# Seam of a feed-forward block and a token mixer: the hand-written order of the splits, and where one head's query weights are loaded and cast

## The chip, the cores and the metric

The kernel runs on one core of a Trainium2 chip. The metric is the device time of one execution in microseconds (us). The engines are named as the profile names them: PE (matrix multiply; PEld is its weight load), DVE (vector), ACT (scalar), POOL (GpSimd, here only issuing DMAs that add into their target) and SP (issues the other DMAs). SBUF is the on-chip memory, PSUM the matmul accumulator with eight banks.

## The reference

One layer on x of shape 512 x 1024, all in float32:

```python
x = x + 0.5 * swiglu(rmsnorm(x, ffn1_norm), ffn1_w_gate, ffn1_w_up, ffn1_w_down)    # D_FF = 2816
x = x + token_mixer(rmsnorm(x, mix_norm), w_in, w_out, ...)
x = x + 0.5 * swiglu(rmsnorm(x, ffn2_norm), ffn2_w_gate, ffn2_w_up, ffn2_w_down)
return rmsnorm(x, final_norm)
```

The mixer projects the normed x by w_in to queries, keys and values of four differential heads (two softmax maps each) and eight dilated heads, attends with a bucketed position bias, and projects by w_out.

## The kernel before

**Numbers.** Every float32 operand of a matmul is split into a high part (rounded to the PE's format) and a low part (the rest). A product is three matmuls: high x high, high x low, low x high (`mm3`, L178 to L180). Such a split is one ACT instruction for the high part and one DVE instruction for the low part, which has to wait for the high part.

**First block.** Gate and up products come first, then the down product in two groups. A group multiplies 2 x 2 blocks by Strassen's scheme: seven products of block sums, and each product runs over the group's pairs of rows. The last down group has six pairs, so 42 operations, numbered 0 to 41, of 6 matmuls each (two token tiles, 128 x 512 outputs). The code's unit of time is `STEP`, one such operation. Weights of operation t are summed on DVE (`total`, L421), cast on ACT (`high`, L453) and the rest is taken on DVE (`low`, L457), nominally 5, 4 and 3 steps ahead. Results of a product are added to x by DVE (L551). Every instruction is an event with a nominal time and a rank; events are emitted in that order, and that is the program order of PE, DVE and ACT, and in this part of SP and POOL too. Each engine works through its own order.

**Closing of the block (`close`).** While the last group runs, events with times relative to its beginning load the first query/key weights of the mixer (`early_load`), split them (`early_high`, `early_low`), square the finished x for the norm (`squared`), form 1/rms (`mean`, `root_part`), scale x (`scaled`), and turn token tiles 0 and 1 by PE transposes (`turn`). A weight set (u, hf) belongs to head u and to one half hf of the eight row blocks k of 128 inputs; a part (u, hf, c) has 512 columns, for two k. Before, (0, 0) and (0, 1) are loaded into `dead` buffers, tiles of the old xh/xl that nobody reads any more, and split within the last group. (1, 0) and (1, 1) are loaded whole into two of the three `raw` buffers, which all other streamed weights use too, and split in the seam.

**The seam (`seam`).** A list of events with times in us puts DVE, ACT and PE work in order, from the end of the group through 16 query/key chunks. Chunks 0 to 3 are u = 0 on the left half of the tokens (token tiles 0 and 1), 4 to 7 are u = 1 on the left half, 8 to 11 and 12 to 15 the same on the right half. A chunk takes two k, for queries and keys: 12 matmuls of 256 columns. Ahead of chunks 4 and 5 PE turns token tiles 2 and 3, whose x needs `summed` (the last product's sums), `squared`, `mean`, `root_part` and `scaled` first. The turned x lies in PSUM, two k in a bank: `xts[side][k // 2]`. `gathered("h", ...)` is the high part of one k on one half (ACT, L1286), `gathered("l", ...)` the low part (DVE, L1288). Chunks with k need both. In the order before, the high parts of side 0 have times of their own and each low part comes 0.45 us behind its high part, so that the list alternates between neighbours:

```python
split(0, (-1.3, -0.9, -0.5, 0.3, 1.0, 1.8, 2.5, 3.2))   # high at t, low at t + 0.45
```

The steps of the mixer's own schedule (`step(c)`) are part of the list too: they load the value weights (`raw_vw`, L165), cast them on ACT (L1409) and take the rest on DVE (L1413) from step 3 on.

Of the kernel before, what the change touches and what calls it, by code (L numbers as in the profile page):

```python
# [14 lines left out]
F32 = mybir.dt.float32  # L15
F32R = mybir.dt.float32r
I32 = mybir.dt.int32
AF = mybir.ActivationFunctionType
# [3 lines left out]
P = 128  # L22
S = 512
D = 1024
FF = 2816
KD = D // P
# [78 lines left out]
STEP = 1410  # L105
# [12 lines left out]
def tile_macaron(ctx: ExitStack, tc, xs, xT, wf, wgu1, wst1, wdg1, wqk, wvw, wv, wo, wgu2, wst2,  # L118
                 wdg2, fg, lams, relb, addc, xn, out):
    nc = tc.nc  # L120
    V, A, G, T = nc.vector, nc.scalar, nc.gpsimd, nc.tensor

    ctx.enter_context(tc.manual_schedule(engines={mybir.EngineType.PE}))
    cp = ctx.enter_context(tc.tile_pool(name="cp", bufs=1))
    sl = ctx.enter_context(tc.tile_pool(name="sl", bufs=1))
    tp = ctx.enter_context(tc.tile_pool(name="tp", bufs=2))
    wp = ctx.enter_context(tc.tile_pool(name="wp", bufs=3))
# [5 lines left out]
    def slot(i, nm, dt=F32):  # L133
        return sl.tile([P, S], dt, tag=f"slot{i}", name=nm)
# [8 lines left out]
    sq = cp.tile([P, S], F32, tag="sq", name="sq")  # L143
# [4 lines left out]
    x = [None] + [cp.tile([P, S], F32, tag=f"x{k}", name=f"x{k}")[:] for k in range(1, KD)]  # L148
# [110 lines left out]
    def ffn(wgu, wst, wdg, n0, n1, norm, early, res, nm, hooks, first=None,  # L259
# [519 lines left out]
        def pipeline():  # L779
# [401 lines left out]
    eps = sp.tile([P, 1], F32, tag="eps", name="eps", bufs=1)  # L1181
    G.memset(eps[:], EPS)
    root = sp.tile([P, 1], F32, tag="root", name="root", bufs=1)
    fin = sp.tile([P, 10 * NQ], F32, tag="fin", name="fin", bufs=1)
    def number(n, tt):
        return fin[:, n * NQ + tt:n * NQ + tt + 1]

    def first_sum(tt):
        V.tensor_scalar(number(2, tt), number(0, tt), 1.0 / D, EPS, op0=ALU.mult, op1=ALU.add)

    def cast(o, a):
        A.copy(o, a)

    def rest(o, a, h):
        V.tensor_tensor(o, a, h.bitcast(F32), op=ALU.subtract)

    closing, early_w, early_raw = {}, {}, {}

    def dead(k):
        return [cp.tile([P, S], F32, tag=f"x{n}{k}", name=f"dead{n}{k}")[:] for n in "hl"]  # L1200

    def early_load(u, hf):
        if u == 0:
            early_raw[u, hf] = dead(1 + 4 * hf)
            for k in range(2):
                nc.sync.dma_start(early_raw[u, hf][k], wqk[u, hf, :, k * 512:(k + 1) * 512])
        else:
            raw = early_raw[u, hf] = wp.tile([P, 1024], F32, tag="raw", name=f"raw_q{u}{hf}")
            nc.sync.dma_start(raw[:], wqk[u, hf])

    def early_source(u, hf, c, n):
        return early_raw[u, hf][:, c:c + n] if u else early_raw[u, hf][c // 512]

    def early_high(u, hf, c, n):
        if u == 0:
            if c == 0 and hf == 0:
                closing[hf] = [tp.tile([P, 5 * HS], F32R, tag="pr0", name=f"wq{n}{hf}")[:, :1024] for n in "hl"]
            elif c == 0:
                tx = tp.tile([P, 12 * HS], F32R, tag="tx", name="wqx", bufs=1)
                closing[hf] = tx[:, :1024], tx[:, 1024:2048]  # L1220
            h, l = [part[:, c:c + n] for part in closing[hf]]
        else:
            h, l = [slot(i, f"wq{n}{u}{hf}{c}", F32R)[:] for n, i in zip("hl", EARLY_SLOTS[u, hf][c // 512])]
        for k in range(n // 256):
            o = slice(k * 256, (k + 1) * 256)
            early_w[u, hf * 4 + c // 256 + k] = h[:, o], l[:, o]
        early_raw[u, hf, c] = h, l
        cast(h, early_source(u, hf, c, n))

    def early_low(u, hf, c, n):  # L1230
        h, l = early_raw[u, hf, c]
        rest(l, early_source(u, hf, c, n), h)

    ys, xts = {}, {}

    def squared(dh, tt):
        if "junk" not in closing:
            closing["junk"] = dead(7)[0]
        junk = closing["junk"] if tt < 2 else sq[:]
        A.activation(junk, x[4 * dh + tt], AF.Square, accum_out=number(dh, tt))  # L1240
        if dh == 0:
            first_sum(tt)

    def scaled(dh, tt):
        y = tp.tile([P, S], F32, tag=("ob", "ptb")[tt % 2], name=f"y{dh}{tt}")
# [15 lines left out]

    def close(at, begin):
        last = begin + 36 * STEP
        todo = [(begin + 9 * STEP, 1.5, early_load, 0, 0), (begin + 11 * STEP, 1.5, early_load, 0, 1),
                (begin + 20.5 * STEP, 5, A.activation, root[:], eps[:], AF.Sqrt),
                (last - 1.8 * STEP, 1.6, early_load, 1, 0),
                (last + 0.4 * STEP, 1.6, early_load, 1, 1)]
        for t, part in ((16.2, (0, 0, 0, 512)), (18.6, (0, 0, 512, 512)), (21.2, (0, 1, 0, 512)), (26.2, (0, 1, 512, 512))):
            todo.append((begin + t * STEP, 4.6, early_high, *part))
            todo.append((begin + (t + 0.9) * STEP, 2.7, early_low, *part))  # L1270
        for tt in range(2):
            todo += [(begin + (25 + 0.5 * tt) * STEP, 4, squared, 0, tt),
                     (last + (0.6 + 0.5 * tt) * STEP, 4, squared, 1, tt),
                     (last + (1.3 + 0.8 * tt) * STEP, 0, mean, tt),
                     (last + (1.6 + 0.8 * tt) * STEP, 0, root_part, tt),
                     (last + (4.4 + 0.6 * tt) * STEP, 4, squared, 1, 2 + tt),
                     (last + (4 + tt) * STEP, 3.9, turn, tt)]
# [24 lines left out]
    def seam(step):  # L1302

        todo, now = [], [0.0]

        def ev(t, f, *a):
            todo.append((t, len(todo), f, a))

        def pe(cost, f, *a):
            ev(now[0], f, *a)  # L1310
            now[0] += cost

        def split(side, highs):
            for k, t in enumerate(highs):
                ev(t, gathered, "h", 1, side, k, xts)
                ev(t + 0.45, gathered, "l", 1, side, k, xts)

        def summed(tt):
            V.scalar_tensor_tensor(x[tt], closing["sums"][tt % 2], 0.5, x[tt], op0=ALU.mult, op1=ALU.add)

        for k in range(1, KD, 2):
            xh[k], xl[k] = [cp.tile([P, S], F32R, tag=f"x{n}{k}", name=f"x{n}{k}m") for n in "hl"]
        ev(-1.5, V.tensor_scalar_mul, sm[:, KD:2 * KD], sm[:, KD:2 * KD], 2.0)
        split(0, (-1.3, -0.9, -0.5, 0.3, 1.0, 1.8, 2.5, 3.2))
        for tt in range(2):
            t = (0.0, 0.9)[tt]
            ev(t, summed, 2 + tt)
            ev(t + 0.6, squared, 0, 2 + tt)
            ev(t + 1.4, mean, 2 + tt)
            ev(t + 1.9, root_part, 2 + tt)  # L1330
            for i in range(2):
                ev(t + 2.6, scaled, i, 2 + tt)
        for t, low, hf, c in ((4.0, 4.7, 0, 0), (5.2, 5.9, 0, 512), (6.6, 7.3, 1, 0), (7.4, 8.1, 1, 512)):
            ev(t, early_high, 1, hf, c, 512)
            ev(low, early_low, 1, hf, c, 512)
        for c in range(16):
            if c in (4, 5):
                pe(0.8, turn, c - 2)
            if c == 5:
                split(1, [now[0] + 0.1 + 0.42 * k for k in range(KD)])  # L1340
# [518 lines left out]
    def step(t):  # L1859
# [272 lines left out]
```

## Time and profile before

| | us |
|---|---|
| median of 3 runs | 916.54 (915.68 to 919.17) |
| the profiled execution | 918.43 |
| its span, first to last instruction | 916.7 |
| mean granted PE clock | 0.999 of full |

| engine | busy us | share of the span |
|---|---|---|
| PE | 906.6 | 99% |
| DVE | 733.4 | 80% |
| ACT | 564.5 | 62% |
| POOL | 101.7 | 11% |

In a timeline row the columns are start (us from the span's start), duration, engine, line, operation, output <- inputs, shapes and count; behind it in brackets stands the idle time of the engine before the row and what ended it. A windows row gives the stretch, its length and the busy time of PE, PEld, DVE, ACT and POOL (with instruction counts), then granted clock, DMA share and GB/s. A row of DMA issues gives target <- source, queue, count, KB each and median us from issue to landing. A count above x1 in a timeline row is of instructions merged into it. The last down group begins at 282.49 us, and the seam's first chunk at 341.46.

### The profile page before, as it was taken

How to read it: one execution, taken by the hardware profiler on the slowest of the kernel's cores; microseconds unless marked ns; L12 is line 12 of the kernel's file. 1: busy time of each engine (PE TensorE's matmuls, PEld its weight loads, DVE VectorE, ACT ScalarE, POOL GpSimd, SP SyncE). 2: the span in 40 equal slices, each digit the busy share in tenths (PEclk: the TensorE clock that was granted, in tenths of full speed). 3: DMA queues.
4: the chain of work that ended last, by engine and by line, in shares of the span. 5: the costliest groups of instructions: out<-in, count | busy, mean ns of one | idle time of the engine just before them, and what ended most of it. 6: DMA issues, size and time to landing. Idle time of an engine off the chain costs nothing.

```text
span 916.7 us, 16048 instructions
## 1 busy us (share of the span) xinstructions
PE 906.6 (99%) x5766; PEld 817.8 (89%) x5766; DVE 733.4 (80%) x1539; ACT 564.5 (62%) x1197; POOL 101.7 (11%) x127
## 2 busy tenths in 40 slices
PE   9999999999999999999999999999999999999997
PEld 7888998899998888888989878989999889999885
DVE  7697998889888876757866546788888888988885
ACT  6345765466567656655776676656666546666673
POOL 0000202121112000000000000010211112112200
PEclk9999999999999999999999999999999999999999
DMA  7464879677889623334444204364788769879902
GB/s 243 127 158 118 212 202 252 149 192 190 202 211 282 159 69 99 93 93 117 137 111 120 69 24 138 93 164 119 202 186 234 178 161 242 205 188 235 258 24 92
DMA packets 68256, 145.47 MB, mean 159 GB/s; under 512 B 7824, under 2 KB 8336, under 8 KB 68176
## 3 DMA queue, kind: packets, MB, share of 16 engines
q1 hardware_dynamic: 51744, 114.34, 39.0%
q0 software_dynamic: 16432, 30.11, 20.5%
q8 instruction: 45, 0.74, 0.3%
q14 instruction: 35, 0.29, 0.1%
HBM read 139.13 MB, written 2.14 MB: 154 GB/s over the span
## 4 chain that ended last, share of the span: by engine, by line
PE 93%; DVE 3%; DMA 2%; ACT 2%; issue 1%; SPq 0%; DVEq 0%; ACTq 0%
PE pt L179 7%; PE pt L180 7%; PE pt L178 7%; PE pwo L178 2%; PE pwo L179 2%; PE pwo L180 2%; PE pua L178 2%; PE pua L180 2%; PE pua L179 2%; PE pq L178 1%; PE pq L179 1%; PE pq L180 1%; PE pk L178 1%; PE pk L180 1%; PE pk L179 1%; PE pga L178 1%
## 5 line engine op out<-in xcount | busy, mean ns | idle before, releaser
L1625 ACT ACTIVATE pr<-pr,mx 128x128 f32<-128x128 f32 (+3 forms) x64 | 36.0, 563 | 36.7 <-DVE mx L1622 36.4
L1622 DVE CUSTOM_DVE_ANT_0 pr<-sc,strip 128x128 f32<-128x128 f32 (+3 forms) x64 | 30.5, 489 | 23.1 <-PE sc L1620 22.6
L551 DVE SCALAR_TENSOR_TENSOR x<-pt,x 128x512 f32<-128x512 f32 x50 | 33.2, 690 | 19.6 <-PE pt L180 12.3
L396 POOL DMA_DIRECT2D s1bg<-wst_dram x10 | 8.6, 862 | 326.7 <-DVE fin L1297 232.5
L457 DVE TENSOR_TENSOR w<-s2b,w 128x512 fp32r<-128x512 f32 x38 | 26.1, 687 | 8.1 <-ACT w L453 8.1
L453 ACT CAST w<-raa 128x512 fp32r<-128x512 f32 x34 | 21.0, 622 | 17.4 <-DVE raa L421 11.7
L453 ACT CAST w<-s2b 128x512 fp32r<-128x512 f32 x38 | 23.6, 620 | 7.0 <-DVE s2b L426 7.0
L453 ACT CAST w<-rab 128x512 fp32r<-128x512 f32 x28 | 17.3, 622 | 16.6 <-DVE rab L421 7.6
L178 PE MATMUL pwo<-w,mh 128*128 128x512 f32 x64 | 25.9, 405 | 0.0
L179 PE MATMUL pwo<-w,mh 128*128 128x512 f32 x64 | 25.0, 391 | 0.0
L180 PE MATMUL pwo<-w,ml 128*128 128x512 f32 x64 | 25.0, 391 | 0.0
L457 DVE TENSOR_TENSOR w<-s2a,w 128x512 fp32r<-128x512 f32 x30 | 20.6, 686 | 3.0 <-ACT w L453 2.8
L457 DVE TENSOR_TENSOR w<-raa,w 128x512 fp32r<-128x512 f32 x34 | 22.8, 686 | 0.0
L1413 DVE TENSOR_TENSOR w<-raw_qk,w 128x512 fp32r<-128x512 f32 x24 | 16.4, 687 | 7.9 <-ACT w L1409 7.8
L453 ACT CAST w<-s2a 128x512 fp32r<-128x512 f32 x30 | 18.6, 620 | 6.6 <-DVE s2a L426 5.8
L179 PE MATMUL pxgb<-ttb,w 128*128 128x256 f32 x80 | 22.5, 281 | 0.0
L396 POOL DMA_DIRECT2D s1ag<-wst_dram x8 | 7.1, 883 | 126.9 <-DMA s3ag<-wst_dram 50.7
L1619 PE MATMUL sc<-k,q 128*128 128x128 f32 (+3 forms) x64 | 20.5, 322 | 0.0
L1620 PE MATMUL sc<-l,q 128*128 128x128 f32 (+3 forms) x64 | 20.2, 322 | 0.0
L179 PE MATMUL pxub<-ttb,w 128*128 128x256 f32 x72 | 20.2, 281 | 0.0
L457 DVE TENSOR_TENSOR w<-rab,w 128x512 fp32r<-128x512 f32 x28 | 18.8, 688 | 0.0
L179 PE MATMUL pwga<-xl,w 128*128 128x256 f32 x64 | 18.0, 281 | 0.0
(1135 smaller groups left out, 3924.7 us busy)
## 6 DMA issues: line engine op xcount, KB each, us to landing
raw_qk<-wqk_dram SPq DMA_DIRECT2D x12, 512.0 KB, 3.6
raw0bg<-wst_dram SPq DMA_DIRECT2D x10, 512.0 KB, 5.1
raw0bu<-wst_dram SPq DMA_DIRECT2D x9, 512.0 KB, 5.7
raw_gua<-wgu_dram SPq DMA_DIRECT2D x8, 512.0 KB, 3.8
raw0ag<-wst_dram SPq DMA_DIRECT2D x8, 512.0 KB, 5.0
strip<-bias_rows SPq DMA_DIRECT2D x16, 256.0 KB, 3.6
raw_wo<-wo_dram SPq DMA_DIRECT2D x8, 512.0 KB, 3.6
raw0au<-wst_dram SPq DMA_DIRECT2D x7, 512.0 KB, 5.8
```

The source lines that it names most:

```text
L178: T.matmul(po, wh, mh, start=first, stop=False, skip_group_check=on)
L179: T.matmul(po, wh, ml, start=False, stop=False, skip_group_check=on)
L180: T.matmul(po, wl, mh, start=False, stop=last, skip_group_check=on)
L396: nc.gpsimd.dma_start(t[:], b, accum_op=ALU.add)
L453: A.copy(made[t][0], source(t))
L457: V.tensor_tensor(l, source(t), h.bitcast(F32), op=ALU.subtract)
L551: V.scalar_tensor_tensor(o, a, f, b, op0=ALU.mult, op1=op1)
L1413: V.tensor_tensor(l[:, c:c + 512], raw[:, c:c + 512], h[:, c:c + 512].bitcast(F32), op=ALU.subtract)
L1619: T.matmul(ps[:, :w], qs[:, qi], ks[:, :w], start=True, stop=False)
L1620: T.matmul(ps[:, :w], qs[:, qi], ls[:, :w], start=False, stop=True)
L1622: V.tensor_tensor_reduce(out=pi, in0=ps[:, :w], in1=st["b"][m][:, w - 1::-1], op0=ALU.add, op1=ALU.min, scale=1.0, scalar=3.0e38, accum_ou ...
L1625: A.activation(pi, pi, AF.Exp, scale=-1.0, bias=st["mx"][:, m, i:i + 1], accum_out=st["ls"][:, m, i:i + 1])
```

## The change

In `close`, the loads of (1, 0) and (1, 1) are cut in halves of 256 KB and three of the four go to dead buffers within the last group: (1, 0, 0) and (1, 0, 1) to the low tiles of k = 3 and 7, (1, 1, 0) to the buffer that (0, 1, 0) had. Only (1, 1, 1) keeps a `raw` buffer. Three of the four splits of u = 1 move from the seam to the last group, at steps 23.6, 28 and 38.5 (high) and 24.5, 28.9 and 39.8 (low); the fourth, (1, 1, 512), stays in the seam ahead of step 4. `EARLY_SLOTS` names other SBUF slots for the results. In `seam`, the front is one list: the two high parts of a bank, then its low parts, with the sums, squares and norm steps of token tiles 2 and 3 between them. `first_sum` becomes an entry of its own, and `dead(k)` hands out one shared pair of tiles for each k. The right half's order is unchanged.

```diff
-EARLY_SLOTS = {(1, 0): ((16, 17), (18, 19)), (1, 1): ((20, 21), (6, 7))}
+EARLY_SLOTS = {(1, 0): ((19, 20), (14, 15)), (1, 1): ((23, 0), (26, 27))}
...
     def dead(k):
-        return [cp.tile([P, S], F32, tag=f"x{n}{k}", name=f"dead{n}{k}")[:] for n in "hl"]
-
-    def early_load(u, hf):
-        if u == 0:
-            early_raw[u, hf] = dead(1 + 4 * hf)
-            for k in range(2):
-                nc.sync.dma_start(early_raw[u, hf][k], wqk[u, hf, :, k * 512:(k + 1) * 512])
+        if ("dead", k) not in closing:
+            closing["dead", k] = [cp.tile([P, S], F32, tag=f"x{n}{k}", name=f"dead{n}{k}")[:] for n in "hl"]
+        return closing["dead", k]
+
+    def early_load(u, hf, k):
+        if (u, hf, k) == (1, 1, 1):
+            r = early_raw[u, hf, k] = wp.tile([P, 1024], F32, tag="raw", name="raw_q")[:, :512]
         else:
-            raw = early_raw[u, hf] = wp.tile([P, 1024], F32, tag="raw", name=f"raw_q{u}{hf}")
-            nc.sync.dma_start(raw[:], wqk[u, hf])
...
+            r = early_raw[u, hf, k] = {(0, 0): dead(1)[k], (0, 1): dead(5)[k], (1, 0): dead((3, 7)[k])[1],
+                                       (1, 1): dead(5)[0]}[u, hf]
+        nc.sync.dma_start(r, wqk[u, hf, :, k * 512:(k + 1) * 512])
...
-        todo = [(begin + 9 * STEP, 1.5, early_load, 0, 0), (begin + 11 * STEP, 1.5, early_load, 0, 1),
-                (begin + 20.5 * STEP, 5, A.activation, root[:], eps[:], AF.Sqrt),
-                (last - 1.8 * STEP, 1.6, early_load, 1, 0),
-                (last + 0.4 * STEP, 1.6, early_load, 1, 1)]
-        for t, part in ((16.2, (0, 0, 0, 512)), (18.6, (0, 0, 512, 512)), (21.2, (0, 1, 0, 512)), (26.2, (0, 1, 512, 512))):
-            todo.append((begin + t * STEP, 4.6, early_high, *part))
-            todo.append((begin + (t + 0.9) * STEP, 2.7, early_low, *part))
+        todo = [(begin + 20.5 * STEP, 5, A.activation, root[:], eps[:], AF.Sqrt)]
+        for t, part in ((9, (0, 0, 0)), (9, (0, 0, 1)), (11, (0, 1, 0)), (11, (0, 1, 1)), (16.5, (1, 0, 0)),
+                        (17.5, (1, 0, 1)), (22.6, (1, 1, 0)), (34.2, (1, 1, 1))):
+            todo.append((begin + t * STEP, 1.5, early_load, *part))
+        for t, low, part in ((16.2, 17.1, (0, 0, 0)), (18.6, 19.5, (0, 0, 512)), (21.2, 22.1, (0, 1, 0)),
+                             (23.6, 24.5, (1, 0, 0)), (26.2, 27.1, (0, 1, 512)), (28, 28.9, (1, 0, 512)),
+                             (38.5, 39.8, (1, 1, 0))):
+            todo.append((begin + t * STEP, 4.6, early_high, *part, 512))
+            todo.append((begin + low * STEP, 2.7, early_low, *part, 512))
...
-        split(0, (-1.3, -0.9, -0.5, 0.3, 1.0, 1.8, 2.5, 3.2))
-        for tt in range(2):
-            t = (0.0, 0.9)[tt]
-            ev(t, summed, 2 + tt)
-            ev(t + 0.6, squared, 0, 2 + tt)
-            ev(t + 1.4, mean, 2 + tt)
-            ev(t + 1.9, root_part, 2 + tt)
-            for i in range(2):
-                ev(t + 2.6, scaled, i, 2 + tt)
-        for t, low, hf, c in ((4.0, 4.7, 0, 0), (5.2, 5.9, 0, 512), (6.6, 7.3, 1, 0), (7.4, 8.1, 1, 512)):
-            ev(t, early_high, 1, hf, c, 512)
-            ev(low, early_low, 1, hf, c, 512)
+        front = ("h0 h1 l0 l1 h2 h3 sum2 l2 l3 h4 h5 sq2 h6 sum3 l4 sq3 first2 mean2 l5 h7 l6 root2 l7 "
+                 "scaled2 first3 mean3 root3 scaled3")
...
+        ev(5.2, early_high, 1, 1, 512, 512)
+        ev(5.9, early_low, 1, 1, 512, 512)
```

In `front`, h and l are the high and low parts of a k on the left half; sum, sq, first, mean, root and scaled belong to token tiles 2 and 3.

More of the change, by code (lines that the diff above doesn't have):

```diff
@@ L1226, in early_high @@
             early_w[u, hf * 4 + c // 256 + k] = h[:, o], l[:, o]
-        early_raw[u, hf, c] = h, l
-        cast(h, early_source(u, hf, c, n))
+        closing[u, hf, c] = h, l
+        cast(h, early_raw[u, hf, c // 512])
     def early_low(u, hf, c, n):
-        h, l = early_raw[u, hf, c]
-        rest(l, early_source(u, hf, c, n), h)
+        h, l = closing[u, hf, c]
+        rest(l, early_raw[u, hf, c // 512], h)
     ys, xts = {}, {}
     def squared(dh, tt):
-        if "junk" not in closing:
-            closing["junk"] = dead(7)[0]
-        junk = closing["junk"] if tt < 2 else sq[:]
+        junk = dead(7)[0] if tt < 2 else sq[:]
         A.activation(junk, x[4 * dh + tt], AF.Square, accum_out=number(dh, tt))
-        if dh == 0:
-            first_sum(tt)
     def scaled(dh, tt):
@@ L1263, in close @@
         last = begin + 36 * STEP
-        todo = [(begin + 9 * STEP, 1.5, early_load, 0, 0), (begin + 11 * STEP, 1.5, early_load, 0, 1),
-                (begin + 20.5 * STEP, 5, A.activation, root[:], eps[:], AF.Sqrt),
-                (last - 1.8 * STEP, 1.6, early_load, 1, 0),
-                (last + 0.4 * STEP, 1.6, early_load, 1, 1)]
-        for t, part in ((16.2, (0, 0, 0, 512)), (18.6, (0, 0, 512, 512)), (21.2, (0, 1, 0, 512)), (26.2, (0, 1, 512, 512))):
-            todo.append((begin + t * STEP, 4.6, early_high, *part))
-            todo.append((begin + (t + 0.9) * STEP, 2.7, early_low, *part))
+        todo = [(begin + 20.5 * STEP, 5, A.activation, root[:], eps[:], AF.Sqrt)]
[7 more added lines that the diff above has]
+            todo.append((begin + low * STEP, 2.7, early_low, *part, 512))
         for tt in range(2):
             todo += [(begin + (25 + 0.5 * tt) * STEP, 4, squared, 0, tt),
+                     (begin + (25 + 0.5 * tt) * STEP, 4, first_sum, tt),
                      (last + (0.6 + 0.5 * tt) * STEP, 4, squared, 1, tt),
@@ L1311, in pe @@
             now[0] += cost
[L1313 to L1316, printed above, removed]
         def summed(tt):
@@ L1323, in seam @@
         ev(-1.5, V.tensor_scalar_mul, sm[:, KD:2 * KD], sm[:, KD:2 * KD], 2.0)
-        split(0, (-1.3, -0.9, -0.5, 0.3, 1.0, 1.8, 2.5, 3.2))
-        for tt in range(2):
-            t = (0.0, 0.9)[tt]
-            ev(t, summed, 2 + tt)
-            ev(t + 0.6, squared, 0, 2 + tt)
-            ev(t + 1.4, mean, 2 + tt)
-            ev(t + 1.9, root_part, 2 + tt)
-            for i in range(2):
-                ev(t + 2.6, scaled, i, 2 + tt)
-        for t, low, hf, c in ((4.0, 4.7, 0, 0), (5.2, 5.9, 0, 512), (6.6, 7.3, 1, 0), (7.4, 8.1, 1, 512)):
-            ev(t, early_high, 1, hf, c, 512)
-            ev(low, early_low, 1, hf, c, 512)
+        front = ("h0 h1 l0 l1 h2 h3 sum2 l2 l3 h4 h5 sq2 h6 sum3 l4 sq3 first2 mean2 l5 h7 l6 root2 l7 "
+                 "scaled2 first3 mean3 root3 scaled3")
+        kinds = {"sum": (summed,), "sq": (squared, 0), "first": (first_sum,), "mean": (mean,), "root": (root_part,)}
+        for n, what in enumerate(front.split()):
+            t, name, k = -1.4 + 0.1 * n, what[:-1], int(what[-1])
+            if name in "hl":
+                ev(t, gathered, name, 1, 0, k, xts)
+            elif name == "scaled":
+                ev(t, scaled, 0, k)
+                ev(t, scaled, 1, k)
+            else:
+                f, *a = kinds[name]
+                ev(t, f, *a, k)
+        ev(5.2, early_high, 1, 1, 512, 512)
+        ev(5.9, early_low, 1, 1, 512, 512)
         for c in range(16):
@@ L1339, in seam @@
             if c == 5:
-                split(1, [now[0] + 0.1 + 0.42 * k for k in range(KD)])
+                for k in range(KD):
+                    ev(now[0] + 0.1 + 0.42 * k, gathered, "h", 1, 1, k, xts)
+                    ev(now[0] + 0.55 + 0.42 * k, gathered, "l", 1, 1, k, xts)
             pe(1.36, step, c)
```

2 lines of the change are left out of this document (removed).

## The prediction

> **What bounds the kernel now.** I read the page's busy time and chain first, then the stretches around the seam, then each engine's timeline there.
>
> ```profile
> PE 906.6 (99%) x5766; PEld 817.8 (89%) x5766; DVE 733.4 (80%) x1539; ACT 564.5 (62%) x1197; POOL 101.7 (11%) x127
> PE 93%; DVE 3%; DMA 2%; ACT 2%; issue 1%; SPq 0%; DVEq 0%; ACTq 0%
> 341.46:349.52 8.06, 7.24 (x49) 6.14 (x48) 5.80 (x21) 5.65 (x15) 0.00 (x0) 1.00 0.01 2
> 357.02:363.63 6.61, 6.11 (x51) 5.91 (x50) 5.71 (x17) 4.66 (x11) 0.00 (x0) 1.00 0.43 149
> ```
>
> The chain is 93% PE, so the change is worth what PE waits for at the seam, and nothing else. Two stretches there show PE short of full (the second number is PE's busy time): the first query chunks on the left half, and the first on the right half. A busy PE may still be late, so I count by pace, from PE's timeline:
>
> ```profile
> 341.46 0.28 PE L178 MATMUL pq<-xh,wqh 128*128 128x256 f32 x1
> 346.42 0.39 PE L179 MATMUL pq<-xl5m,wqx 128*128 128x256 f32 x1 [0.35 <-DVE xl5m L1288]
> 347.80 0.38 PE L179 MATMUL pq<-xl,wqx 128*128 128x256 f32 x1 [0.33 <-DVE xl L1288]
> 349.52 1.03 PE L1260 MATMUL xt<-ident,y 128*128 128x128 f32 x8
> 350.31 0.36 PE L178 MATMUL pq<-xh,wqh 128*128 128x256 f32 x1
> 355.58 0.28 PE L178 MATMUL pq<-xh,wqh 128*128 128x256 f32 x1
> 357.02 0.38 PE L178 MATMUL pq<-xh,wqh 128*128 128x256 f32 x1
> 357.89 0.38 PE L179 MATMUL pq<-xl,wqh 128*128 128x256 f32 x1 [0.50 <-DVE xl L1288]
> 363.63 0.28 PE L178 MATMUL pq<-xh,wqh 128*128 128x256 f32 x1
> ```
>
> A chunk is 12 matmuls, two k: one took 357.02 - 355.58 = 1.44 us, so 0.72 a k and 0.12 a matmul. Chunks 0 to 3 are 48 matmuls, 5.76 us; from 341.46 to the turn at 349.52 they took 8.06. PE lost **2.30 us**, all to xl parts that came late (two of the waits are marked). Chunks 8 to 11, again 48, took 363.63 - 357.02 = 6.61: **0.85 us** lost. A turn takes 350.31 - 349.52 = 0.79 and stays. So 3.15 us is all that this seam can give.
>
> **Why the xl parts are late.**
>
> ```profile
> 339.99 0.47 ACT L1286 ACTIVATE xh1m<-xt,x 128x256 fp32r<-128x256 f32 x1
> 340.35 0.47 ACT L1286 ACTIVATE xh<-xt,x 128x256 fp32r<-128x256 f32 x1
> 341.79 0.47 ACT L1286 ACTIVATE xh3m<-xt,x 128x256 fp32r<-128x256 f32 x1 [0.97 <-DVE xl L1288]
> 342.45 0.63 ACT L1240 ACTIVATE sq<-x 128x512 f32<-128x512 f32 x1 [0.18 <-DVE x L1319]
> 340.49 0.48 DVE L1288 SCALAR_TENSOR_TENSOR xl<-xt,x,xh 128x256 fp32r<-128x256 f32 x1 [1.60 <-ACT xh1m L1286]
> 340.89 0.47 DVE L1288 SCALAR_TENSOR_TENSOR xl1m<-xt,x,xh1m 128x256 fp32r<-128x256 f32 x1
> 341.28 0.47 DVE L1288 SCALAR_TENSOR_TENSOR xl<-xt,x,xh 128x256 fp32r<-128x256 f32 x1
> 341.68 0.68 DVE L1319 SCALAR_TENSOR_TENSOR x<-pt,x 128x512 f32<-128x512 f32 x1
> 346.74 0.21 DVE L1297 SCALAR_TENSOR_TENSOR fin<-fin 128x1 f32<-128x1 f32 x1
> 347.27 0.48 DVE L1288 SCALAR_TENSOR_TENSOR xl<-xt,x,xh 128x256 fp32r<-128x256 f32 x1
> ```
>
> k = 2 and 3 share a PSUM bank. The list of before has the low part of 2 ahead of the high part of 3, and xh3m starts at 341.79, just after that xl ends (341.28 + 0.47 = 341.75): ACT stood 0.97 us for a bank that both engines only read. In the same way xl (k = 0) starts at 340.49, when xh1m of its bank ends (340.46). So work on one bank runs in list order across the two engines; every alternation costs a hand-over.
>
> **The one list, step by step.** Pitches from these rows: a high 0.36 (339.99 to 340.35), a low 0.40 (340.49 to 340.89), a square 0.63, a sum (L1319) 0.68 less an overlap of 0.08, about 0.60, a root part 0.53 (346.74 to 347.27). Nothing ahead of h0 moves (next part), so h0 to h5 run through on ACT without a hand-over, to about 341.9: of each bank both highs now stand first. DVE: l0 340.49, l1 340.89, then sum2. Its start is bounded by DVE being free, 341.28, and by the only row there is, 341.68; I take 341.68. Then l2 342.28, l3 342.67, sum3 343.06 to 343.74, l4 343.66. ACT: sq2 after sum2 at 342.39, h6 343.02, sq3 after sum3 at 343.77, the root's Sqrt at 344.45, h7 344.56 to 345.03. DVE: l5 344.32, l6 345.06 to 345.54, root2, l7 345.96 to 346.44, scaled2 to 346.83; y of the fourth token tile by 348.8. PE asks for xl of k at 341.46 + 0.72 k + 0.12: k = 2 at 343.02 (ready 342.76), k = 3 at 343.74 (343.15), k = 5 at 345.18 (344.80), k = 6 at 345.90 (345.54), k = 7 at 346.62 (346.44). All in time, the last by 0.18; with sum2 at 341.28 by 0.58. The turns would be at 347.22 and 349.53, and their y are there. The 2.30 go; for a margin of 0.18 and hand-overs I give back 0.15, between 0 and 1.2 (rival 1).
>
> The Trainium skill's "PSUM — Partial Sum Buffer", section "PSUM bank collisions raise a hardware error", says that two engines may not touch one bank at once, reads against reads included, so that software has to order them; another bank is free. The trace agrees with the first half (0.97 us at xh3m). By it sum2 need not wait for PE's work on the other sum bank and would start at 341.28, and the sum would be 3.15 where the row gives 3.0.
>
> **The three splits moved into the down group.** The high of (1,0,0), (1,0,512) and (1,1,0) go to ACT, the lows to DVE, at nominal steps 23.6 to 39.8. What they cost and the holes for them:
>
> ```profile
> 348.76 0.61 ACT L1192 CAST wqh<-raw_q 128x512 fp32r<-128x512 f32 x1
> 350.45 0.69 DVE L1195 TENSOR_TENSOR wql<-raw_q,wqh 128x512 fp32r<-128x512 f32 x1 [0.35 <-ACT wqh L1192]
> 282.49 0.40 PE L178 MATMUL pt<-w,h0a 128*128 128x512 f32 x1
> 331.49 0.39 PE L178 MATMUL pt<-w,h1a 128*128 128x512 f32 x1
> 314.01 0.62 ACT L453 CAST w<-sCa 128x512 fp32r<-128x512 f32 x1 [0.54 <-PE pt L180]
> 322.85 1.37 DVE L551 SCALAR_TENSOR_TENSOR x<-pt,x 128x512 f32<-128x512 f32 x2 [2.05 <-PE pt L180]
> 320.81 0.62 ACT L453 CAST w<-sBa 128x512 fp32r<-128x512 f32 x1 [0.73 <-DVE w L457]
> 337.13 0.72 ACT L1248 ACTIVATE y<-x,fin 128x512 f32<-128x512 f32 x1 [0.68 <-DVE fin L1300]
> ```
>
> 36 operations lie between the two PE rows: a step is 49.00 / 36 = 1.361 us. The first high stands right ahead of the cast at 314.01, in a hole of 0.54, with a pitch of about 0.52; the second in the one of 0.73 ahead of 320.81; the third ahead of y at 337.13, in a hole of 0.68. The first two lows shift DVE's casts by up to 1.4, and the hole of 2.05 ahead of 322.85 takes them; those casts serve operations two or three steps (2.7 to 4.1 us) later. The third low lies before l0, in its hole of 1.60. So on the path: 0, bounds 0 and 0.69, if one doesn't fit. With the cover gone, each would cost its 0.69. In the seam they free 3 x 0.61 on ACT and 3 x 0.69 on DVE behind scaled3, where only the last split (1,1,512) stays; its weights are asked for at about 353, it ends near 350.
>
> **The loads.** Each 512 KB load becomes two of 256 KB, so two more issues on SP.
>
> ```profile
> 296.39 0.43 SPq L1206 DMA_DIRECT2D deadl<-wqk_dram  x1
> 311.54 5.47 SPq L1172 DMA_DIRECT2D strip<-bias_rows  x4
> 329.67 4.28 SPq L1209 DMA_DIRECT2D raw_q<-wqk_dram  x2
> 351.17 0.33 SPq L165 DMA_DIRECT2D raw_vw<-wvw_dram  x1
> deadl<-wqk_dram SPq DMA_DIRECT2D x2, 256.0 KB, 10.0
> strip<-bias_rows SPq DMA_DIRECT2D x8, 256.0 KB, 3.4
> raw_vw<-wvw_dram SPq DMA_DIRECT2D x4, 512.0 KB, 4.9
> 355.96 0.62 ACT L1409 CAST w<-raw_vw 128x512 fp32r<-128x512 f32 x1 [3.97 <-DMA raw_vw<-wvw_dram]
> 356.49 0.47 ACT L1286 ACTIVATE xh<-xt,x 128x256 fp32r<-128x256 f32 x1
> ```
>
> SP issued nothing between 296.8 and 311.54, so (1,0,0) and (1,0,1), into buffers that are already dead, go at about 297 and land by 307 (10.0 us, as the crowded deadl), 6 us ahead of the cast near 313.5. (1,1,0) waits for the low that frees its buffer, near 313; behind it on SP stand the strips and the last loads, none of them wanted before 335. (1,1,1) takes the one raw buffer that raw_q took at 329.67.
>
> Here is the second gain. Before, two raw_q held two of the three raw buffers, and the second raw_vw was issued only at 351.17, when a low had freed one; ACT stood 3.97 us for it, and the xh at 356.49, the first of the right half, stood behind that cast. That is the 0.85. With one raw_q, the second raw_vw gets a buffer near 335.8 and lands by 341. The right half's highs then start near 350.8, right after the turn and four casts; its l0 is ready near 351.7 and asked for at 354.8. **0.85 gone**; bounds 0.6 and 0.85. Third and fourth raw_vw come 2 to 3 us earlier too.
>
> The new slots are asked for only after their last reader in the group, and the shared dead tiles and the first_sum entries change no work: 0.
>
> **Sum.** -2.30 + 0.15 - 0.85 = **-3.0 us**. The profiled execution took 918.43 (span 916.7 and 1.73 outside it): 915.4. The median of the runs shown, 916.54, lies 1.89 below it: **913.5 us**.
>
> **The rivals.**
> 1. *The list's tail is late.* sq2 and sq3 now stand ahead of h6 and h7, and l6 waits for h7. Four hand-overs lie between sum2 and l7; were each 0.3 longer (the low at 350.45 waited 0.35 for its cast), l7 would end at 346.44 + 1.2 = 347.64, 1.0 after PE asks. For it: the margin of 0.18. Against: the hand-overs seen at 340.49 and 341.79 took 0.03 to 0.04. Gain 2.0: 914.5.
> 2. *Nothing is gained.* The chain takes the 3 us back in the attention behind, or the splits weren't what held PE. For: ACT and DVE stand in 5% of the chain. Against: PE is 99% busy, and what follows the seam starts from PE's order. 916.5.
> 3. *Slower: ACT stands for a load.* ACT takes its queue in order; the row at 355.96 shows a cast that waits for its load with everything behind it. If SP issues the strips first, the two loads leave after 317.0 (311.54 + 5.47) and land at L = 320.4 (3.4 us) to 327.0 (10.0). Behind the first high stands the cast at 314.01, of operation 28, due on PE at 282.49 + 28 x 1.361 = 320.6; it would be ready at L + 0.52 + 0.62 + 0.69 + about 0.2, so PE stands for L - 318.6: 1.8 to 8.4 us. It outweighs the gain from L = 321.6. In the middle, 5.1, the kernel is 2.1 slower: 918.6; at the far end 5.4: 921.9. For: nothing on SP forces the order written. Against: the strips wait for their own slots until 311.54, 14 us after these loads could go.
>  The Trainium skill's "DMA: Bandwidth & Descriptors", section "Issuing engines are not separate DMA queues", has loads of all queues share the same 16 engines; by it the far end is the likelier one where loads are thick. The trace agrees: 10.0 us near 296 and 3.4 for the strips, of the same 256 KB.
>
> **How the numbers follow.** Forecast 0.74, rival 1 0.12, rival 2 0.06, rival 3 0.08. This kernel's measurement tells about 0.5% from no change, 4.6 us. The forecast, rivals 1 and 2 and the near half of rival 3 lie within it; more than 3.15 isn't in the seam, so faster by over 0.5% is left to what I don't see: 0.04. Slower: the far half of rival 3 and the unseen, 0.08. Same: 0.88. The range: from 3.15 us gained and 1.6 of spread in the runs shown (915.68 to 919.17), 911.8, to rival 2 and 1 us of spread, 917.5.
>
> **What would show it.** In the changed profile: xh3m without its wait on xl; chunks 0 to 3 in under 6.0 us; the first matmuls of the right half without a wait; the second raw_vw issued near 336; w casts in the down group where they were. A wait of ACT on a wqk load near 313, or of PE's pt on a w cast between 320 and 338, would speak for rival 3; l7 later than 346.6 for rival 1. I am wrong if PE's waits at the seam go and the span doesn't fall with them, or if they stay.

## The result, and the profile after

The changed kernel took **912.71 us** (median of 6 runs, 912.20 to 913.22) against 916.25 for the kernel before in the same session. The medians differ by 3.5 us. The ratio, 0.9957 with a 95% interval of 0.9944 to 0.997, is that of the means and gives 3.9 us less, between 2.7 and 5.1. In a later session, five runs gave 913.06 against 916.61, ratio 0.9967 [0.9956, 0.9979]. Forecast were 913.5 and "within 0.5%".

First the page and the two stretches of the seam that were short of PE in the kernel before (windows rows, as in the prediction):

```profile
PE 902.2 (99%) x5766; PEld 815.4 (90%) x5766; DVE 733.2 (81%) x1539; ACT 564.6 (62%) x1197; POOL 101.9 (11%) x127
PE 98%; DVE 1%; ACT 0%; DMA 0%; issue 0%; DVEq 0%; SPq 0%; ACTq 0%
339.00:344.74 5.74, 5.74 (x49) 5.74 (x48) 5.06 (x17) 3.65 (x11) 0.00 (x0) 1.00 0.01 3
352.22:357.98 5.76, 5.76 (x50) 5.76 (x49) 2.24 (x10) 0.85 (x3) 0.00 (x0) 1.00 0.30 98
```

The chain is PE to 98%, where it was 93%. Chunks 0 to 3 take 5.74 us instead of 8.06, chunks 8 to 11 take 5.76 instead of 6.61, and in both PE is busy for the whole stretch. PE's timeline, with the rows that bound the accounts below (first matmul of the last down group, first chunk, the two turns, chunks 8 and 12, last matmul):

```profile
280.06 0.40 PE L178 MATMUL pt<-w,h0a 128*128 128x512 f32 x1
339.00 0.28 PE L178 MATMUL pq<-xh,wqh 128*128 128x256 f32 x1
344.74 1.04 PE L1254 MATMUL xt<-ident,y 128*128 128x128 f32 x8
347.04 1.04 PE L1254 MATMUL xt<-ident,y 128*128 128x128 f32 x8
352.22 0.28 PE L178 MATMUL pq<-xh,wqh 128*128 128x256 f32 x1
357.98 0.28 PE L178 MATMUL pq<-xh,wqh 128*128 128x256 f32 x1
903.50 0.39 PE L180 MATMUL pt<-kxb,h2b 128*128 128x512 f32 x1
```

The two profiled executions differ by more than the change is worth: 918.43 before, 912.50 after, spans 916.7 and 910.7. Where the 6 us lie:

- Ahead of the last down group, where the code is the same: 282.49 - 280.06 = 2.43 us. This is no gain of the change (see the last experiments).
- From the group's first matmul to chunk 12, the seam: 363.63 - 282.49 = 81.14 before, 357.98 - 280.06 = 77.92 after. **3.22 us**, the change. All but 0.03 of it lies behind the start of the first chunk: the down group up to there took 58.97 and 58.94.
- From chunk 12 to the last matmul: 546.00 before (to 909.63), 545.52 after. The second profiled run of the changed kernel has 546.27 there (357.77 to 904.04), so this 0.5 is spread between runs (545.51 to 546.27 over the twelve traces of this study).

Now the front's order on ACT and DVE:

```profile
337.89 0.47 ACT L1283 ACTIVATE xh<-xt,x 128x256 fp32r<-128x256 f32 x1
338.25 0.48 ACT L1283 ACTIVATE xh3m<-xt,x 128x256 fp32r<-128x256 f32 x1
340.98 0.63 ACT L1236 ACTIVATE sq<-x 128x512 f32<-128x512 f32 x1 [0.30 <-DVE x L1311]
347.86 0.47 ACT L1283 ACTIVATE xh<-xt,x 128x256 fp32r<-128x256 f32 x1
338.43 0.48 DVE L1285 SCALAR_TENSOR_TENSOR xl1m<-xt,x,xh1m 128x256 fp32r<-128x256 f32 x1
338.82 0.68 DVE L1311 SCALAR_TENSOR_TENSOR x<-pt,x 128x512 f32<-128x512 f32 x1
343.11 0.48 DVE L1285 SCALAR_TENSOR_TENSOR xl7m<-xt,x,xh7m 128x256 fp32r<-128x256 f32 x1
```

xh3m follows its neighbour at the pitch of 0.36 without a wait; before it stood 0.97. The first sum (338.82) starts when DVE is done with xl1m, though PE's last matmul of the group (in the other sum bank) had begun only at 338.76. xl7m, the last part of the left half, ends at 343.59; PE uses it at 344.14.

Loads and casts:

```profile
294.64 2.75 SPq L1210 DMA_DIRECT2D deadl<-wqk_dram  x3
310.80 0.33 SPq L1210 DMA_DIRECT2D deadh<-wqk_dram  x1
333.35 0.33 SPq L165 DMA_DIRECT2D raw_vw<-wvw_dram  x1
310.92 0.61 ACT L1192 CAST wqh<-deadl 128x512 fp32r<-128x512 f32 x1
346.82 1.14 ACT L1406 CAST w<-raw_vw 128x512 fp32r<-128x512 f32 x2
```

The second raw_vw is issued at 333.35, before the first chunk (before: 351.17, behind the turn), no cast waits for it, and the right half's first xh follows at 347.86. The three loads at 294.64 are those of (0, 1, 1), (1, 0, 0) and (1, 0, 1), issued between 294.64 and 297.39; the one at 310.80 is (1, 1, 0). The cast of (1, 0, 0) runs at 310.92 without a wait for its load.

### The profile page after: what moved, and what is told of

Its sections match the earlier page's. It is cut to its first block, busy times and chain, and to the rows that moved or that the text cites. A ratio compares the mean times of both kernels' runs of the same rounds, so it can differ in the third digit from the quotient of the medians.

```text
span 910.7 us, 16054 instructions
## 1 busy us (share of the span) xinstructions
PE 902.2 (99%) x5766; PEld 815.4 (90%) x5766; DVE 733.2 (81%) x1539; ACT 564.6 (62%) x1197; POOL 101.9 (11%) x127
## 4 chain that ended last, share of the span: by engine, by line
PE 98%; DVE 1%; ACT 0%; DMA 0%; issue 0%; DVEq 0%; SPq 0%; ACTq 0%
PE pt L178 8%; PE pt L180 8%; PE pt L179 8%; PE pq L178 2%; PE pwo L178 2%; PE pq L180 2%; PE pk L178 2%; PE pq L179 2%; PE pk L180 2%; PE pk L179 2%; PE pwo L180 2%; PE pwo L179 2%; PE pua L178 2%; PE pua L180 2%; PE pua L179 2%; PE pga L178 1%
## 5 line engine op out<-in xcount | busy, mean ns | idle before, releaser
L453 ACT CAST w<-s2b 128x512 fp32r<-128x512 f32 x38 | 23.6, 620 | 7.9 <-DVE s2b L426 7.9
L396 POOL DMA_DIRECT2D s1ag<-wst_dram x8 | 7.1, 883 | 120.8 <-ACT xh L296 39.8
```

Source lines behind the costliest of these rows:

```text
L396: nc.gpsimd.dma_start(t[:], b, accum_op=ALU.add)
L453: A.copy(made[t][0], source(t))
```

## The experiments

"Seam" is the time from the first matmul of the last down group to chunk 12, read from each trace. The ratios are to the kernel before, with 95% intervals. The first four kernels ran beside the 916.53 of the kernel before, the ones with 4 warm-ups and with one late load beside 916.58, the others beside 916.61.

| kernel | median us (range) | ratio | seam us |
|---|---|---|---|
| before | 916.53, 916.61 and 916.58 in three sessions | | 81.14 |
| list alone | 914.41 (913.72-915.11) | 0.9976 [0.9967, 0.9986] | 79.36 |
| moved splits alone | 914.40 (914.14-917.23) | 0.9985 [0.9976, 0.9993] | 80.28 |
| before, one cast later | 915.31 (914.55-917.23) | 0.9988 [0.9979, 0.9996] | 80.25 |
| after, alternating list | 914.13 (913.68-917.03) | 0.9980 [0.9971, 0.9989] | 79.46 |
| after again | 913.06 (912.68-914.40) | 0.9967 [0.9956, 0.9979] | 77.93 |
| after, three late loads | 921.44 (919.73-923.46) | 1.0055 [1.0042, 1.0067] | 85.08 |
| after, one late load | 912.95 (912.74-913.69) | 0.9958 [0.9946, 0.9971] | 77.92 |
| after, 9 warm-ups | 912.85 (912.70-913.20) | 0.9962 [0.9950, 0.9974] | 77.93 |
| after, 10 warm-ups | 913.00 (912.37-913.25) | 0.9960 [0.9947, 0.9973] | 77.92 |
| after, 4 warm-ups | 914.73 (913.88-915.07) | 0.9974 [0.9963, 0.9985] | 77.94 |

The medians gain more than the seam: the moved splits alone 2.1 us where their seam gains 0.86, the cast put later 1.2 for 0.89. The traces of kernels with eight warm-ups differ by up to 2.65 us ahead of the down group (279.84 to 282.49) and by 0.8 behind chunk 12, where their code is the same, and each single edit has one traced run. So the single edits are told apart by the seam, and the medians only say that each is faster than before.

**The new list alone**, on the kernel before; loads, splits of u = 1 and slots stay as they were.

```diff
-        split(0, (-1.3, -0.9, -0.5, 0.3, 1.0, 1.8, 2.5, 3.2))
...
+        front = ("h0 h1 l0 l1 h2 h3 sum2 l2 l3 h4 h5 sq2 h6 sum3 l4 sq3 first2 mean2 l5 h7 l6 root2 l7 "
+                 "scaled2 first3 mean3 root3 scaled3")
```

> The front of the seam is the new list; the loads and splits of u = 1 are those of before (two raw buffers, all four splits in the seam). Theory A, the prediction's sum (two separate gains of 2.30 and 0.85 us): PE loses nothing in chunks 0 to 3 and the kernel is 2.3 us faster than before. Theory B, the wait is handed on: PE comes to chunk 4 about 2.3 us sooner, but the first split of u = 1 still stands behind scaled3 on ACT, which moves by only some 0.5 us; PE then waits about 1.6 us for the weights of chunk 4, and 2 to 3 us at chunk 8, where the cast of the second raw_vw still waits for its load. The kernel is then 0.3 to 0.8 us faster than before.

PE's and ACT's timelines (chunk 0, the turn, chunk 4, the second turn, chunk 8; then the value cast):

```profile
339.38 0.28 PE L178 MATMUL pq<-xh,wqh 128*128 128x256 f32 x1
345.12 1.04 PE L1258 MATMUL xt<-ident,y 128*128 128x128 f32 x8
346.83 0.39 PE L178 MATMUL pq<-xh,wqh 128*128 128x256 f32 x1 [0.67 <-ACT wqh L1192]
348.85 1.03 PE L1258 MATMUL xt<-ident,y 128*128 128x128 f32 x8
354.03 0.28 PE L178 MATMUL pq<-xh,wqh 128*128 128x256 f32 x1
352.02 0.62 ACT L1409 CAST w<-raw_vw 128x512 fp32r<-128x512 f32 x1 [2.64 <-DMA raw_vw<-wvw_dram]
```

Chunks 0 to 3 take 5.74 instead of 8.06: the list by itself takes the whole loss there. PE then reaches chunk 4 sooner than the split of (1, 0, 0), which stands behind scaled3 in the seam: from turn to turn 348.85 - 345.12 = 3.73 us against 347.04 - 344.74 = 2.30 with the splits moved, so 1.43 is lost again, where theory B expected 1.6. The wait at chunk 8 went as well, which theory B didn't expect, although ACT's cast still stood 2.64 us for its load: counted from the down group's start the cast came 1.88 us sooner (71.59 instead of 73.47), chunk 8 only 0.93 (73.60 instead of 74.53). So the seam gains 1.78, and neither sum came out. Part of it is not the list's work: of the 1.88 us, the load was issued only 0.54 sooner (348.57 here, 351.17 before, each from its own group's start), and the rest is that it landed 3.4 us after its issue here and 4.8 in the trace of before. The first xl of the right half was ready 0.25 us before PE asked for it (353.90 against 354.15). By these numbers a landing as late as before would have cost about 1.1 us at chunk 8, and the gain would be about 0.7, as theory B has it; this is an estimate, no run shows it.

**The moved splits alone**: the changed kernel with the front order of before.

```diff
-        front = ("h0 h1 l0 l1 h2 h3 sum2 l2 l3 h4 h5 sq2 h6 sum3 l4 sq3 first2 mean2 l5 h7 l6 root2 l7 "
...
+        for k, t in enumerate((-1.3, -0.9, -0.5, 0.3, 1.0, 1.8, 2.5, 3.2)):
+            ev(t, gathered, "h", 1, 0, k, xts)
+            ev(t + 0.45, gathered, "l", 1, 0, k, xts)
```

> Loads and splits of u = 1 as in the change, the front of the seam in the order of before. A (separate gains): chunks 0 to 3 lose their 2.30 us as before, chunk 8 waits for nothing: 0.85 us faster than before. B (handed on): the same 0.85, because what is moved lies behind the front; the two parts alone would then give 1.2 to 1.7 together, and the change gives 3.2.

```profile
338.83 0.28 PE L178 MATMUL pq<-xh,wqh 128*128 128x256 f32 x1
343.80 0.39 PE L179 MATMUL pq<-xl5m,wqx 128*128 128x256 f32 x1 [0.36 <-DVE xl5m L1285]
345.18 0.38 PE L179 MATMUL pq<-xl,wqx 128*128 128x256 f32 x1 [0.33 <-DVE xl L1285]
346.91 1.04 PE L1254 MATMUL xt<-ident,y 128*128 128x128 f32 x8
```

Chunks 0 to 3 take 8.08, with the two waits of before to 0.01 us. The wait at chunk 8 is gone. The seam gains 0.86, the 0.85 of the prediction, as both theories expected.

**What held chunk 8**: the kernel before with the mixer's second value cast in step 7 instead of 5, nothing else.

```diff
-    for n, c in enumerate((3, 5)):
+    for n, c in enumerate((3, 7)):
```

> The kernel before with one edit: the second value-weight unit is due at step 7 and no longer at step 5, so that its cast on ACT stands behind the right half's highs. If that cast's wait for its load is what holds chunk 8: the wait of PE at chunk 8 (0.85 us) goes, and the kernel is 0.85 us faster than before. If something else holds the highs (the turn, the bank): no change, 0.

```profile
349.67 0.47 ACT L1286 ACTIVATE xh<-xt,x 128x256 fp32r<-128x256 f32 x1 [0.26 <-PE xt L1260]
353.81 0.62 ACT L1409 CAST w<-raw_vw 128x512 fp32r<-128x512 f32 x1 [1.47 <-DMA raw_vw<-wvw_dram]
```

ACT's xh now waits only for PE's turn, the cast still waits for its load, but behind seven of the xh parts, and PE has no wait at chunk 8. The seam gains 0.89. The load itself is not faster here (the cast starts 5.2 us after its issue, 4.8 before); that the cast no longer stands ahead of the xh parts is the whole of it.

**Is it the banks?** The changed kernel with a list that alternates within each bank. ACT's own order and DVE's own order are those of the changed kernel; only how the two interleave differs.

```diff
-        front = ("h0 h1 l0 l1 h2 h3 sum2 l2 l3 h4 h5 sq2 h6 sum3 l4 sq3 first2 mean2 l5 h7 l6 root2 l7 "
+        front = ("h0 l0 h1 l1 h2 sum2 l2 h3 l3 h4 sum3 l4 h5 sq2 h6 sq3 first2 mean2 l5 l6 h7 root2 l7 "
```

> The changed kernel with another order of the list across engines: each low of a bank's first k stands ahead of the high of its second k (h0 l0 h1 l1 and so on). The order on ACT alone and on DVE alone is the same as in the changed kernel. If work on one bank runs in list order across engines: each h1, h3, h5, h7 waits for the low of its neighbour, xl5 comes 1.2 to 1.4 us after PE asks, and the kernel is 1.0 to 1.9 us slower than the changed one, so 1.3 to 2.2 faster than before. If the gain came from the engines' own orders: no difference from the changed one, 3.2 to 3.5 us faster than before.

```profile
338.30 0.48 ACT L1283 ACTIVATE xh1m<-xt,x 128x256 fp32r<-128x256 f32 x1 [0.55 <-DVE xl L1285]
340.32 0.48 ACT L1283 ACTIVATE xh3m<-xt,x 128x256 fp32r<-128x256 f32 x1 [1.18 <-DVE xl L1285]
342.34 0.47 ACT L1283 ACTIVATE xh5m<-xt,x 128x256 fp32r<-128x256 f32 x1 [1.18 <-DVE xl L1285]
344.25 0.39 PE L179 MATMUL pq<-xl5m,wqx 128*128 128x256 f32 x1 [0.92 <-DVE xl5m L1285]
```

ACT stands for DVE's xl ahead of the second part of the first three banks, xl5m comes to PE at 344.25, 1.4 us after it asks (339.12 + 0.72 x 5 + 0.12), and the seam is 79.46 - 77.93 = 1.53 us longer than with the list by banks. Both orders only read the bank. So 1.53 of the 2.32 us at chunks 0 to 3 hang on how the two engines alternate, with no change of the order within either. The other 0.8 isn't isolated by any run: the order of before also has the sums, squares and norm steps at other places.

**After again**, as the mark for a later session.

> The changed kernel again, unaltered, on the same chip and beside the same runs of the kernel before as the next three: the mark they are measured against. Expected 3 to 4.5 us faster than the kernel before (about 912.5), with chunks 0 to 3 at 5.74 us and chunks 8 to 11 at 5.76 on the matrix engine, whatever the theory.

Seam 77.93, as in the first trace.

**The price of rival 3**: the changed kernel with three early loads behind all four strips on SP.

```diff
-        for t, part in ((9, (0, 0, 0)), (9, (0, 0, 1)), (11, (0, 1, 0)), (11, (0, 1, 1)), (16.5, (1, 0, 0)),
-                        (17.5, (1, 0, 1)), (22.6, (1, 1, 0)), (34.2, (1, 1, 1))):
+        for t, part in ((9, (0, 0, 0)), (9, (0, 0, 1)), (11, (0, 1, 0)), (11, (0, 1, 1)), (24.37, (1, 0, 0)),
+                        (24.36, (1, 0, 1)), (24.35, (1, 1, 0)), (34.2, (1, 1, 1))):
...
-(21.2, 22.1, (0, 1, 0)), (23.6, 24.5, (1, 0, 0))
+(21.2, 24.3, (0, 1, 0)), (24.4, 25.3, (1, 0, 0))
```

> The changed kernel with the three early loads put behind all four strips of the down group on SyncE's queue, and the split of part (1,0,0) set so that its cast on ScalarE is called for a little after them. Theory A (rival 3 of the prediction was priced rightly, its case just did not come up): the load issues near 315 us, lands at L between 319 and 320.5, ScalarE's cast stands for it, the cast of x2 behind it is late, and the matrix engine loses about L-317.5, that is 1.5 to 3 us inside the down group; the time is that much above the changed kernel's, 914 to 916. Theory B (the down group has slack enough to swallow a cast that waits): the cast shows a wait of 1 to 3 us, the matrix engine shows no idle time, and the time stays within 0.5 us of the changed kernel's.

SP's issues and how long they took to land, the cast, DVE behind it, PE's first matmuls of the next operation and the first one back at the old pace, and a windows row of the slow stretch:

```profile
315.32 0.90 SPq L1210 DMA_DIRECT2D deadl<-wqk_dram  x2
deadl<-wqk_dram SPq DMA_DIRECT2D x2, 256.0 KB, 5.5
321.35 0.62 ACT L1192 CAST wqh<-deadl 128x512 fp32r<-128x512 f32 x1 [9.08 <-DMA deadl<-wqk_dram]
323.15 0.15 DVE L1189 TENSOR_SCALAR fin<-fin 128x1 f32<-128x1 f32 x1 [7.64 <-ACT deadh L1236]
319.38 0.39 PE L180 MATMUL pt<-w,h4a 128*128 128x512 f32 x1
322.55 0.79 PE L178 MATMUL pt<-w,xl 128*128 128x512 f32 x1 [2.77 <-ACT w L453]
324.71 0.80 PE L179 MATMUL pt<-w,xl 128*128 128x512 f32 x1 [1.37 <-DVE w L457]
329.45 0.39 PE L178 MATMUL pt<-w,h3a 128*128 128x512 f32 x1
325.00:329.00 4.00, 4.00 (x10) 3.13 (x10) 3.97 (x8) 3.02 (x6) 0.00 (x0) 0.50 0.00 0
```

The late loads cost 8.4 us by the medians and 7.16 by the seam, far over the 1.5 to 3 expected. The traced run was the fastest of the six (919.73; the slowest took 923.46), so what the others lost beyond the 7.16 isn't shown. One cast that waits is what starts it. At the usual pitch of 0.23 the first matmul was due at 319.61 and came 2.94 late; the second was due 0.23 behind it and came another 1.93 late, because DVE's low part stood behind norm steps that waited for ACT's squares, and these stood behind the cast. The rest is pace: from 324.71 to 329.45 eleven matmuls took 4.74 us where 11 x 0.228 = 2.51 is usual, 2.23 lost, with a granted clock of 0.50 in the windows row. 2.94 + 1.93 + 2.23 = 7.10.

**One late load.** As above, with the same later split, but only part (1, 0, 0) is loaded later.

```diff
-(11, (0, 1, 1)), (16.5, (1, 0, 0)),
+(11, (0, 1, 1)), (24.37, (1, 0, 0)),
...
-(21.2, 22.1, (0, 1, 0)), (23.6, 24.5, (1, 0, 0))
+(21.2, 24.3, (0, 1, 0)), (24.4, 25.3, (1, 0, 0))
```

> The changed kernel with only the load of part (1,0,0) behind all four strips; the other two early loads go where the change puts them. The load is issued near 315 us alone and lands at L about 318.7; then ScalarE's cast stands until L, the matrix engine's first matmul of the next weight starts at L+1.2 and its second, which waits for VectorE's low half behind two of ScalarE's sums of squares, at L+3.4 (both distances as with three late loads, where L was 321.35), against 319.6 and 319.8 asked for. Theory A (the lost time is these waits, and the slow pitch of 0.43 that followed them with three late loads needs a longer standstill than the 2 us here): 2 to 2.5 us above the changed kernel's, about 915, all matmuls after the wait at a pitch of 0.23. Theory B (a standstill of 2 us is enough for the slow pitch): 2.2 us more, about 917, and twelve matmuls at 0.43.

```profile
310.37 0.43 SPq L1210 DMA_DIRECT2D deadl<-wqk_dram  x1
310.90 3.65 SPq L1172 DMA_DIRECT2D strip<-bias_rows  x3
314.09 0.62 ACT L1192 CAST wqh<-deadl 128x512 fp32r<-128x512 f32 x1 [1.91 <-DMA deadl<-wqk_dram]
```

The edit didn't do what was expected of it: the load was issued behind one strip (three follow it), not four, and L was 314.1 instead of 318.7. So it doesn't tell the two theories on the pace apart. It gives another point: a cast that stands 1.91 us for its load here costs PE nothing (seam 77.92), since the work behind it isn't due until 319.6.

**The start of the run.** Three kernels with 9, 10 and 4 instead of 8 warm-up matmuls (`WARM`, L37) ahead of the first real one.

```diff
-WARM = 8
+WARM = 9
```

> The changed kernel with nine instead of eight warm-up matmuls ahead of the first real one. It concerns the 2.43 us by which the two profiled runs of before and after differed ahead of the change, where the first twelve 512-column matmuls ran at a pitch of 0.43 us in one run and 0.23 in the other. Theory A (the slow pitch comes from the gap of about 0.5 us between the warm-up and the first real matmul, and strikes only some runs): the gap goes, all runs start at the quick pitch, the median falls by 0 to 1 us and the spread of the runs narrows. Theory B (the slow pitch has nothing to do with the gap): the spread stays as it was, and the median is the same or, where the ninth delays the first real matmul, up to 0.3 us later.

> The same with ten warm-up matmuls, which delay the first real one by about 0.4 us. Theory A (the pace at the start depends on how long the matrix engine has been busy without a gap): the quick pitch in every run, a narrow spread, and the median 0.4 us above that of nine at most. Theory B (it does not): the median 0.4 us above that of the changed kernel with the same spread.

> The changed kernel with four instead of eight warm-up matmuls, so that the matrix engine stands idle for about 2.4 us (2.9 to 5.3) before its first real one. Theory A (idle time just ahead of the first real matmul sets the slow pitch of 0.43 us for some 5 us): the first twelve or more 512-column matmuls at 0.43 in the trace and in nearly every run, the median 2 to 3 us above the changed kernel's, 915 to 916. Theory B (the slow pitch of the kernel before's profiled run was an accident that idle time has no part in): the first matmuls at 0.23 and the median within 0.5 us of the changed kernel's.

The second and third real matmul of PE's timeline, in the kernel before (8 warm-ups), after (8) and with 4, in this order; with 4 also the first one, and the first of the down group:

```profile
6.00 0.63 PE L1132 MATMUL pua<-eha,w 128*128 128x512 f32 x1
6.42 0.63 PE L1132 MATMUL pga<-eha,w 128*128 128x512 f32 x1
```

```profile
5.60 0.40 PE L1132 MATMUL pua<-eha,w 128*128 128x512 f32 x1
5.84 0.40 PE L1132 MATMUL pga<-eha,w 128*128 128x512 f32 x1
```

```profile
5.01 0.79 PE L1132 MATMUL pga<-eha,w 128*128 128x512 f32 x1 [1.94 <-ACT w L1112]
5.60 0.63 PE L1132 MATMUL pua<-eha,w 128*128 128x512 f32 x1
6.03 0.63 PE L1132 MATMUL pga<-eha,w 128*128 128x512 f32 x1
282.60 0.40 PE L178 MATMUL pt<-w,h0a 128*128 128x512 f32 x1
```

With four warm-ups the first 14 matmuls run at the slow pitch of 0.43, and the down group begins at 282.60, beside 282.49 in the profiled run of the kernel before. In the ten other traces of this study it begins between 279.84 and 280.43. So the 2.43 us ahead of the change are this slow start (but for 0.15, by which the first real matmul came later, 5.41 against 5.26), which the profiled run of the kernel before happened to have with eight warm-ups. By the medians, four warm-ups cost 1.7 us (914.73 against 913.06), less than the 2 to 3 expected; against the 912.95 of one late load in the same session it is 1.8. Nine or ten give the median of eight; a narrower range is seen (0.5 and 0.9 us wide, beside 1.7), which five runs don't prove. None of the kernels tried beats the changed one by more than its spread.

## Why the prediction was right, point by point

- **The terms.** Chunks 0 to 3 were to give back 2.30 and gave 2.32 (8.06 to 5.74). Chunks 8 to 11 were to give 0.85 and gave 0.85. The 0.15 taken off for margins and hand-overs was not needed. The seam's 3.22 stands against 3.0. The single edits bear the two terms out: list alone 2.32 at chunks 0 to 3, splits alone 0.86. Of the miss of 0.8 in the time (913.5 against 912.71), 0.2 is the seam; 0.3 is the median of before, 916.25 with six runs where three had given 916.54; and the last 0.3 lies outside the seam, where the code is the same.
- **Mis-sized: the start of sum2**, the sum of token tile 2. Of the two bounds I took the row of before (341.68 in its time, 0.4 later) and not DVE being free. It started when DVE was free. l7 therefore had a margin of 344.14 - 343.59 = 0.55, where the bounds said 0.18 and 0.58. The Trainium skill's "PSUM — Partial Sum Buffer", section "PSUM bank collisions raise a hardware error", which leaves other banks free, was the better guide here: 338.82 beside PE's 338.76 in the other bank.
- **Bank order as the cause** was argued from one wait of 0.97. The alternating list shows it by itself: up to 1.18 on ACT per bank, 1.53 on PE. The prediction has no other cause for the 2.30; for the remaining 0.8 that stays argued.
- **The loads**: (1, 1, 0) at 310.80 and the second raw_vw at 333.35 are 313.2 and 335.8 in the time of before (2.43 later), forecast "near 313" and "near 335.8". (1, 0, 0) and (1, 0, 1) left some 2 us later than the "about 297" of the forecast (298.9 and 299.5), and the cast of (1, 0, 0) still had no wait. The right half's first xh came 8.86 us after the first chunk (347.86 - 339.00), forecast 9.34. The deciding step, that the cast's wait and not PE's work held chunk 8, is shown by the kernel with that cast alone put later. How large the term is hangs on the landing of one load, which took 3.4 to 5.2 us in the traces with that wait; that the sum had 0.85 to the hundredth is in part luck.
- **Splits in the down group at 0**: the group took 58.94 instead of 58.97. The kernel with the list alone shows what they are for: without the move, 1.43 of the list's 2.32 are lost again at chunk 4. The prediction added the two edits' gains as if either could be had alone; it didn't say that the list needs the move. They give 1.78 and 0.86 alone and 3.22 together, in one trace each, and the 1.78 has a quicker landing in it.
- **From profile to median.** The prediction carried 918.43 over to the median by a difference of 1.89 that it did not explain. The slow start, by which the profiled run was 2.4 us longer, is the likely reason; the runs behind the median aren't traced. The sum doesn't hang on it, since it took its 3.0 off the median.
- **Rivals.** Rival 1 fell: of the waits between sum2 and l7 on which l7 depends, the longest shown is the 0.30 ahead of the second square. Rival 2 fell: from chunk 12 on both kernels take 546 within the spread. Rival 3 didn't come up, since these loads left by 297.39 and the first strip at 309.09, 11 us later, but its price was too low: the kernel with three late loads had L = 321.35, 323.7 in the time of before, just the middle that was priced at L - 318.6 = 5.1 and 918.6. The waits were 4.87; the pace added 2.23 that no term held, and it took 921.44. Of that, the trace shows 7.16 over the changed kernel. Its two loads landed 5.5 us after they were issued (median), between the bounds of 3.4 and 10.0.

## What to carry to other kernels

Where two engines read one PSUM bank, give each its whole turn: both parts of the one engine, then both of the other; and look what the engine that now comes sooner will ask for next, since over half of such a gain was lost at the next wait here (1.43 of 2.32). A cast that waits for its load holds all that stands behind it on ACT, so put it behind the work that PE needs, or free its buffer earlier. Before a difference of two profiles is read, compare them at a point ahead of the change.

## What the runs showed of the hardware

PE's pace after standing still was not expected. In the kernel with three late loads PE stood 2.77 us by the profile's row (2.94 by its pitch). The matmul at 322.55, right behind it, already took 0.79 us. After the second wait (1.93) 512-column matmuls ran 0.43 apart instead of 0.23 until 329.14, with a granted clock of 0.50 from 325 to 329. At the start of a run the same 0.43 was seen for some 5 us, with the granted clock at 1.00 in the windows row of that stretch, so that row doesn't show it; whether eight warm-ups prevent it changes from run to run.

```profile
5.00:10.50 5.50, 5.09 (x12) 4.03 (x13) 2.89 (x6) 3.81 (x9) 0.00 (x0) 1.00 1.00 338
```

(Kernel before: 12 matmuls in 5.5 us; after has 23 there.) The Trainium skill's "TensorE: Matmul & The Clock Gate", section "Part 1: The HAM clock gate (the "warmup" mystery)", names this: half the clock, 426.7 ns for 512 columns, until a free-running window of about 3.4 us was busy, and again after an idle one. The pace agrees (0.43), and so does the change from run to run at the start. The idle time doesn't quite: 2.77 us were enough here.
